# Weight loads two chunks ahead of the modulation blocks, and blocks moved behind LayerNorm, in a two-layer trunk

## The chip, the cores and the metric

The kernel runs on one core of a Trainium2 chip. The metric is the time of one execution on the device in microseconds, as the median of several runs. The profile is of one such execution; its times are counted from the first instruction.

The engines have these short names: PE is TensorE (PEld its weight loads), DVE is VectorE, ACT is ScalarE, POOL is GpSimd, SP is SyncE, which here issues all DMAs, in its program's order. Each engine runs its own list of instructions in order and waits at semaphores for the others.

## What is computed

Two layers of a trunk over 512 tokens of width 2048, in float32. Each layer:

```
mod = silu(c) @ ada_w[l] + ada_b[l]; shift, scale, gate = split(mod, 3)
h = rms_norm(x, norm_g[l]) * (1 + scale) + shift
z = h @ w_in[l]          # q-latent | kv-latent | rope key | MLA gate | conv input (2x) | conv gate
mla_out  = attention(q, k, v) * silu(mla_gate)        # 8 heads, low rank q and kv, causal
u = val * sigmoid(u_gate); u = depthwise_conv31(u)
u = silu(layer_norm(u)) @ w_pw[l] + b_pw[l]
conv_out = u * silu(conv_gate)
x = x + gate * (concat(mla_out, conv_out) @ w_out[l])
```

What matters here: `mod` is a product of a vector of 2048 with a matrix of 2048 x 6144 per layer. It needs 48 MB of weights in each layer and is done on VectorE. Of its 48 blocks of 128 values, blocks 0 to 15 are the shift, 16 to 31 the scale and 32 to 47 the gate, each for one chunk of 128 features.

## The kernel before

Features lie on the partitions in 16 chunks of 128, and tokens along the free axis, 512 of them. Products keep float32's precision: weights and activations are split into a high half (rounded to the matmul's format) and a low half (the rest), and each product takes three matmuls, high by high (L249), high by low (L250) and low by high (L251). Weights come as raw tiles of 512 KB (`load_w`, L228, four buffers). `split_w` (L235) makes the high half with a cast on ScalarE (L242, five buffers `hi`) and the low half with a subtraction (L243, five buffers `lo`), on GpSimd in most places; in the second layer's pointwise and output products (`PENG`, L94) on VectorE.

**A modulation block** (`Gemv.block`, L332) loads one block of 128 x 2048 weights (1 MB, tensor `ada`) and multiplies and sums it on VectorE in one instruction (L336), whose result is one column of `mod`. There are three buffers for these in the first layer's input product and two (`GB`) in the later stages. `make_h` (L352) makes a chunk of `h`: VectorE scales x (L356), ScalarE adds the shift and rounds (L357), VectorE makes the low half (L358).

**The input product of the first layer** (L442 to L459) goes over chunks of `h`: three for the first eight output tiles, then eight for the gate tiles `mg`, then the other thirteen for the first eight. `modulate_to` (L434) makes the chunks of `h` that the next step needs, with two blocks each, and `chunk` (L397) then loads 512 KB of weights, splits them and does 24 matmuls. **In the second layer** (L485 to L494) a chunk of `h` needs no block of its own at first; 14 blocks that the first layer left over (`LATE`) are done between the chunks, from the list `todo`.

**Behind attention** (L870 on), with the convolution's results ready, come the conv gate's product `cg` (8 tiles), the pointwise product `pw` (8 tiles) and the output product `wo` (16 tiles). LayerNorm's steps over the convolution are spread between the steps of `cg`: `ln_mean` (L876), `ln_center` (L881: subtract the mean, square on ScalarE, add into `vacc`), the token sums of `vacc` by matmuls (`st`, L194), the reciprocal root, `crs`, and `ln_silu` (L889), LayerNorm's last stage. `more(n)` (L910) puts blocks of `todo` between these: one per tile of `cg` once any instruction of LayerNorm is noted in `ln_ins`, one in each of the first six steps of `pw` behind the split of `cat`, and the rest at an even `rate` in the first 15 steps of `wo`. 34 blocks are done in this part in the first layer, 16 in the second.

The order in which instructions stand is set by a scheduler that takes the program's order and the dependences; `tc.issue_after(x)` holds an instruction behind x.

```
raw = load_w(src, 8, P)
for q in (0, 4):
    hi, lo = split_w(raw[:, q:q + 4], SENG)
    for n in range(4):
        mm3(tiles[q + n], hi[:, n], lo[:, n], hj[:, 0], hj[:, 1], start, stop)
```

Of the kernel before, what the change touches and what calls it, by code (L numbers as in the profile page):

```python
# [16 lines left out]
P = 128  # L17
S = 512
D = 2048
KC = D // P  # L20
NT = S // P
DEPTH = 2
H = 8
# [27 lines left out]
def hybrid_trunk(ctx, tc, xT, c, pos, invf, vec, adaT, w_s, w_t, w_kr, w_q, w_kv, w_pw, w_o, outT):  # L51
    nc = tc.nc
    V, A, T = nc.vector, nc.scalar, nc.tensor
# [16 lines left out]
    def nm(s):  # L70
        uid[0] += 1
        return f"{s}_{uid[0]}"
# [17 lines left out]
    AHEAD, NRAW, NHI, NLO = 2, 4, 5, 5  # L90
# [8 lines left out]
    K1, KH = 3, 8  # L99
# [6 lines left out]
    def psum(tag, n):  # L106
        return pp.tile([P, S], F32, tag=tag, bufs=NB[tag], name=nm(n))
# [11 lines left out]
    def ms(n):  # L119
        return f2(n, "m", NM)  # L120
# [107 lines left out]
    def load_w(src, a, b):  # L228

        raw = wp.tile([P, 1024], F32, tag="raw", bufs=NRAW, name=nm("raw"))  # L230
        rawv = raw[:, :a * b].rearrange("p (a b) -> p a b", a=a)
        nc.sync.dma_start(out=rawv, in_=src)
        return rawv
# [154 lines left out]
    def layer(l, xs, rstd, rpsum):  # L388
        last = l == DEPTH - 1
# [4 lines left out]

        tags = [t for t in ("mm", "up", "s", "cv", "pz") for _ in range(NB[t])]

        def chunk(tiles, src, hj, start, stop):  # L397
            raw = load_w(src, 8, P)
            for q in (0, 4):
                hi, lo = split_w(raw[:, q:q + 4], SENG)  # L400
                for n in range(4):
                    mm3(tiles[q + n], hi[:, n], lo[:, n], hj[:, 0], hj[:, 1], start, stop)
# [14 lines left out]
        def w_first(j):  # L417
            return w_s[l, j].rearrange("p (a b) -> p a b", a=8)

        h, part = [], [None] * H  # L420
        if l == 0:
            def modulated(j):
                if j >= EARLY:
                    scale0(j)
                g.block(0, j)
                h.append(make_h(0, j, xs[j], rstd if j else rpsum[0]))

            def park(tiles, where):
                for n in range(8):
                    p = where(n)  # L430
                    (A.copy if n % 2 else V.tensor_copy)(out=p, in_=tiles[n])
                    yield p

            def modulate_to(m):  # L434
                while len(h) < min(int(m), KC):
                    if len(h) < NI:
                        with tc.issue_after(rstd_ins.ins):
                            modulated(len(h))
                    else:
                        modulated(len(h))  # L440

            first = [psum(t, "z") for t in tags]  # L442
            for j in range(K1):
                modulate_to(j + 1)
                chunk(first, w_first(j), h[j], j == 0, j == K1 - 1)
            held = list(park(first, lambda n: ms("held") if n < 2 else f2("held", "held", 6, sp)))
            mg = [psum(t, "z") for t in tags]
            for j in range(KH):
                modulate_to(max(j + 1, K1 + MR0 * (j + 1)))
                chunk(mg, w_t[l, 0:H, :, j, :].rearrange("a p b -> p a b"), h[j], j == 0, j == KH - 1)  # L450
            part = list(park(mg, lambda n: ms("part")))
            first = [psum(t, "z") for t in tags]
            for j in range(K1, KC):
                modulate_to(max(j + 1, K1 + MR0 * KH + MR * (j + 1 - K1)))
                chunk(first, w_first(j), h[j], j == K1, j == KC - 1)
            krw = kr_weights()
            for n in range(8):
                V.tensor_add(out=held[n], in0=first[n], in1=held[n])
                first[n] = held[n]  # L459
        else:  # L460


            ws = []
            for j in range(2):
                raw = load_w(w_first(j), 8, P)
                ws.append([split_w(raw[:, q:q + 4], SENG, extra[0] if j and q else None) for q in (0, 4)])
                h.append(r4("h"))
            first = [psum(t, "z") for t in tags[:7]]

            def early(n, tk):  # L470
                for j in range(2):
                    hi, lo = ws[j][n // 4]
                    mm3(first[n][:, tk], hi[:, n % 4], lo[:, n % 4], h[j][:, 0, tk], h[j][:, 1, tk], j == 0, False)

            for i, (tk, rs) in enumerate(zip(HALF, rpsum)):
                for j in range(2):
                    make_h(l, j, xs[j], rs if j == 0 else rstd[:, tk], h[j], tk)
                for j in range(2):
                    for n in range(7):
                        hi, lo = ws[j][n // 4]  # L480
                        mm3(first[n][:, tk], hi[:, n % 4], lo[:, n % 4], h[j][:, 0, tk], h[j][:, 1, tk], i == 0 and j == 0, False)
            first.append(psum(tags[7], "z"))
            early(7, slice(0, S))
            h_ins = bc_ins[1]
            for j in range(2, KC):  # L485

                while len(todo) > max(KC, KC + 2 * (KC - LATE) - (j - 1) - max(0, min(2, j - 3))):
                    with tc.issue_after(h_ins.ins):
                        _, b = todo[0]
                        gemv[0].block(*todo.pop(0))  # L490
                        if b < KC:
                            make_gs(l, b)
                h.append(make_h(l, j, xs[j], rstd))
                chunk(first, w_first(j), h[j], False, j == KC - 1)  # L494
            krw = kr_weights()


# [375 lines left out]
        mean, vacc, crs = ms("mean"), ms("vacc"), ms("crs")  # L873
        ctile, ln_ins = [], [None]
# [6 lines left out]
        def ln_center(j):  # L881
            if j % 2 == 0:
                t = bp.tile([P, 2, S], F32, tag="c", bufs=4, name=nm("c"))
                nc.sync.dma_start(out=t, in_=cd[j // 2])
                ctile.extend((t[:, 0], t[:, 1]))
            ln_ins[0] = V.tensor_sub(out=ctile[j], in0=ctile[j], in1=mean)
            square_sum(vacc, ctile[j], j)

        def ln_silu(j):  # L889
# [35 lines left out]
        for j in range(NCC):  # L925
            for _ in range(4):
                ws.step()
                bg(VBUD)
            if ln_ins[0] is not None:
                with tc.issue_after(ln_ins[0].ins):  # L930
                    more(1)
        bg(1e9)
# [9 lines left out]
        def cat_split(src, t=None):  # L942
            t = r4("cat") if t is None else t
            A.copy(out=t[:, 0], in_=src)  # L944
            cat_ins[0] = V.tensor_sub(out=t[:, 1], in0=src, in1=f(t[:, 0]))  # L945
            return t
# [11 lines left out]
        for j in range(NCC):  # L958
            ws.step()
            ws.step()  # L960
            if j < 6:

                t = bp.tile([P, 2, S], F32R, tag="c", bufs=4, name=nm("cat")) if j < 4 else None
                cat[j] = cat_split(mout[j], t)
                with tc.issue_after(cat_ins[0].ins):
                    more(1)
        for j in (6, 7):
# [139 lines left out]
```

## Time and profile before

| | |
|---|---|
| median of 3 runs | 1667.66 us (1665.26 to 1672.59) |
| the profiled execution | 1668.02 us |
| its span, first to last instruction | 1666.2 us |
| TensorE busy | 1581.1 us (95%) |
| VectorE busy | 1226.2 us (74%) |
| ScalarE busy | 687.4 us (41%) |
| GpSimd busy | 659.7 us (40%) |
| granted clock of TensorE, mean | 0.987 |
| moved by DMA | 271.53 MB, mean 163 GB/s |

A matmul's shown duration overlaps the next one's, so TensorE counts as busy also where it is slow; how fast it goes is seen from the number of matmuls in a stretch, or from the distance of their starts. The chain of waits that ends last has 62% of its time on TensorE and 28% on VectorE, where the largest line is the block's, L336, with 7% of the span. The share of the granted clock is 1 at 2.4 GHz and 0.5 at 1.2 GHz.

### The profile page before, as it was taken

The page shows a single profiled execution, that of the slowest core. Times are in us where ns is not written, and L with a number is a line of the kernel's source. Part 1 is how long each engine was busy: PE and PEld are TensorE (multiplying, and loading weights), DVE is VectorE, ACT ScalarE, POOL GpSimd, SP SyncE. Part 2 cuts the span into 40 slices and gives each one's busy share as a digit, 9 for nine tenths or more (in the row PEclk, how much of TensorE's full clock was granted, in tenths as well). Part 3 has the DMA queues.
Part 4 walks back from the last instruction along what each step waited for, and adds up shares of the span by engine and source line. Part 5 has one row for each costly group of instructions (what it writes and reads, how often), then busy time and mean ns, then how long its engine had stood idle before and what let it go on. Part 6 is the DMA issues. An engine that isn't in the chain of part 4 may idle for free.

```text
span 1666.2 us, 20654 instructions
## 1 busy us (share of the span) xinstructions
PE 1581.1 (95%) x7350; PEld 1300.9 (78%) x7350; DVE 1226.2 (74%) x2008; ACT 687.4 (41%) x1284; POOL 659.7 (40%) x440
## 2 busy tenths in 40 slices
PE   4988999999999989999999899999999998999999
PEld 2766778877888878788887678888787887888888
DVE  8898897889999558766549675777788787784332
ACT  4222455554654335322223264545445443532221
POOL 2565633425233455666625554331434335100000
PEclk9999999999999999999999999999999999999999
DMA  8877323223233644898936613322332355565441
GB/s 304 287 278 286 135 90 100 70 83 86 76 114 98 231 152 167 287 335 296 322 98 228 246 64 108 92 92 80 99 93 70 104 170 211 177 236 198 151 142 62
DMA packets 82890, 271.53 MB, mean 163 GB/s; under 512 B 10721, under 2 KB 21729, under 8 KB 70241
## 3 DMA queue, kind: packets, MB, share of 16 engines
q1 hardware_dynamic: 82786, 270.20, 48.1%
q8 instruction: 58, 0.95, 0.2%
q14 instruction: 46, 0.38, 0.1%
HBM read 257.55 MB, written 12.62 MB: 162 GB/s over the span
## 4 chain that ended last, share of the span: by engine, by line
PE 62%; DVE 28%; ACT 6%; issue 3%; DMA 1%; POOL 1%; SPq 0%; POOLq 0%; ACTq 0%; DVEq 0%
DVE ada L336 7%; PE wo L250 7%; PE wo L251 7%; PE wo L249 7%; DVE cv L547 5%; PE z L249 4%; PE z L251 4%; PE z L250 4%; PE cg L249 3%; PE cg L251 3%; PE cg L250 3%; PE mg L251 2%; PE mg L249 2%; PE mg L250 2%; DVE x L356 2%
## 5 line engine op out<-in xcount | busy, mean ns | idle before, releaser
L243 POOL TENSOR_TENSOR lo<-raw,hi 128x512 fp32r<-128x512 f32 x380 | 595.2, 1581 | 657.5 <-ACT hi L242 647.3
L242 ACT CAST hi<-raw 128x512 fp32r<-128x512 f32 (+1 forms) x512 | 307.1, 611 | 518.0 <-PE wo L250 209.6
L547 DVE SCALAR_TENSOR_TENSOR cv<-u,lvec,cv 128x512 f32<-128x512 f32 x464 | 348.6, 751 | 7.4
L249 PE MATMUL z<-h,hi 128*128 128x512 f32 (+1 forms) x782 | 305.8, 396 | 17.2 <-ACT h L357 11.0
L251 PE MATMUL z<-h,lo 128*128 128x512 f32 (+1 forms) x782 | 305.8, 391 | 8.3 <-POOL lo L243 8.3
L250 PE MATMUL z<-h,hi 128*128 128x512 f32 (+1 forms) x782 | 304.6, 390 | 0.8 <-DVE h L358 0.7
L336 DVE CUSTOM_DVE_ANT_0 ada<-ada,cb,avec 128x2048 f32<-128x2048 f32 x96 | 257.4, 2682 | 40.5 <-DMA ada<-in_adaT_dram 40.4
L249 PE MATMUL wo<-cat,hi 128*128 128x512 f32 (+1 forms) x544 | 205.8, 378 | 2.0 <-ACT cat L944 2.0
L250 PE MATMUL wo<-cat,hi 128*128 128x512 f32 (+1 forms) x544 | 206.3, 379 | 1.1 <-DVE cat L945 1.0
L251 PE MATMUL wo<-cat,lo 128*128 128x512 f32 (+1 forms) x544 | 205.8, 378 | 0.0
L249 PEld LDWEIGHTS z<-h,hi 128*128 128x128 f32 x782 | 148.5, 191 | 49.2 <-ACT h L357 13.4
L251 PEld LDWEIGHTS z<-h,lo 128*128 128x128 f32 x782 | 148.4, 190 | 42.9 <-POOL lo L243 13.3
L250 PEld LDWEIGHTS z<-h,hi 128*128 128x128 f32 x782 | 148.6, 190 | 29.3 <-DVE h L358 1.8
L243 DVE TENSOR_TENSOR lo<-raw,hi 128x512 fp32r<-128x512 f32 (+1 forms) x132 | 86.3, 655 | 95.0 <-ACT hi L242 94.7
L249 PEld LDWEIGHTS wo<-cat,hi 128*128 128x128 f32 x544 | 102.9, 189 | 21.2 <-ACT cat L944 2.4
L250 PEld LDWEIGHTS wo<-cat,hi 128*128 128x128 f32 x544 | 102.9, 189 | 21.2 <-DVE cat L945 2.3
L251 PEld LDWEIGHTS wo<-cat,lo 128*128 128x128 f32 x544 | 103.0, 189 | 18.8
L249 PE MATMUL cg<-h,hi 128*128 128x512 f32 x256 | 103.0, 402 | 0.0
L250 PE MATMUL cg<-h,hi 128*128 128x512 f32 x256 | 101.5, 397 | 0.0
L251 PE MATMUL cg<-h,lo 128*128 128x512 f32 x256 | 101.5, 396 | 0.0
L780 ACT ACTIVATE pr<-pr,smx,sc 128x128 f32<-128x128 f32 (+1 forms) x64 | 41.9, 654 | 122.8 <-DVE smx L779 122.7
L357 ACT ACTIVATE h<-x,mod 128x512 fp32r<-128x512 f32 (+1 forms) x34 | 23.3, 697 | 136.8 <-DVE mod L336 100.5
(265 smaller groups left out, 2543.4 us busy)
## 6 DMA issues: line engine op xcount, KB each, us to landing
ada<-in_adaT_dram SPq DMA_DIRECT2D x96, 1024.0 KB, 5.7
raw<-in_w_t_dram SPq DMA_DIRECT2D x120, 512.0 KB, 3.8
raw<-in_w_o_dram SPq DMA_DIRECT2D x64, 512.0 KB, 4.6
raw<-in_w_s_dram SPq DMA_DIRECT2D x32, 512.0 KB, 5.9
raw<-in_w_pw_dram SPq DMA_DIRECT2D x16, 512.0 KB, 3.6
raw<-in_w_q_dram SPq DMA_DIRECT2D x24, 256.0 KB, 2.7
x<-in_xT_dram SPq DMA_DIRECT2D x8, 512.0 KB, 6.8
kf<-kfd SPq DMA_DIRECT2D x16, 256.0 KB, 3.7
```

The source lines that it names most:

```text
L242: A.copy(out=hiv, in_=rawv)
L243: i = eng.tensor_tensor(out=lov, in0=rawv, in1=f(hiv), op=ALU.subtract)
L249: T.matmul(out=ps, lhsT=whi, rhs=mhi, start=start, stop=False)
L250: T.matmul(out=ps, lhsT=whi, rhs=mlo, start=False, stop=False)
L251: T.matmul(out=ps, lhsT=wlo, rhs=mhi, start=False, stop=stop)
L336: V.tensor_tensor_reduce(out=t, in0=t, in1=self.cb, scale=1.0, scalar=vv(l, "ada_b", b), op0=ALU.mult, op1=ALU.add, accum_out=mods[l][:, b ...
L356: V.scalar_tensor_tensor(out=x, in0=x, scalar=gs(l, j), in1=rstd, op0=ALU.mult, op1=ALU.mult)
L357: A.activation(out=hi, in_=x, func=AF.Identity, bias=shift(l, j))
L547: V.scalar_tensor_tensor(out=box[-1], in0=u[:, k:k + S], scalar=w, in1=box[0], op0=ALU.mult, op1=ALU.add)
L780: A.activation(out=pr[:, :n], in_=pr[:, :n], func=AF.Exp, scale=scl, bias=nb, accum_out=sums)
```

## The change

Three things change.

1. Weights of the input products are loaded ahead. A list `to_come` holds the loads still to be issued, in order, and `come(n)` issues them until `n` loaded tiles stand ready. In the first layer `come(AHEAD)`, with `AHEAD` = 2, is called ahead of the blocks of each new chunk of `h` (but the first), in the second ahead of the blocks of each chunk from the third on. `chunk` takes the oldest loaded tile.
2. `ln_center` no longer notes its instruction in `ln_ins`, so the blocks in `cg` begin behind the first `ln_silu`. In the second layer there are none in `cg`.
3. In the pointwise product the first layer's blocks stand in steps 1 to 5 instead of 0 to 5, and the second layer has none. As `rate` shares out what is left, the first layer's output product gets 28 blocks instead of 24, and the second's 16, all that there are.

```diff
-        def chunk(tiles, src, hj, start, stop):
-            raw = load_w(src, 8, P)
+        raws, to_come = [], []
+
+        def come(n):
+
+            while to_come and len(raws) < n:
+                raws.append(load_w(to_come.pop(0), 8, P))
+
+        def chunk(tiles, hj, start, stop):
+            come(1)
+            raw = raws.pop(0)
...
                     else:
+                        come(AHEAD)
                         modulated(len(h))
 
+            to_come += [w_first(j) for j in range(K1)]
+            to_come += [w_t[l, 0:H, :, j, :].rearrange("a p b -> p a b") for j in range(KH)]
+            to_come += [w_first(j) for j in range(K1, KC)]
...
-                chunk(first, w_first(j), h[j], j == 0, j == K1 - 1)
+                chunk(first, h[j], j == 0, j == K1 - 1)
...
             h_ins = bc_ins[1]
+            to_come += [w_first(j) for j in range(2, KC)]
             for j in range(2, KC):
+                come(AHEAD)
...
-            ln_ins[0] = V.tensor_sub(out=ctile[j], in0=ctile[j], in1=mean)
+            V.tensor_sub(out=ctile[j], in0=ctile[j], in1=mean)
...
-            if ln_ins[0] is not None:
+            if ln_ins[0] is not None and not last:
                 with tc.issue_after(ln_ins[0].ins):
                     more(1)
...
                 cat[j] = cat_split(mout[j], t)
+            if 0 < j < 6 and not last:
                 with tc.issue_after(cat_ins[0].ins):
                     more(1)
```

Where the instructions now stand, at three places.

VectorE, first layer, the end of the sum over LayerNorm's squares (`vacc`), up to the first use of its token sums (`st`); before, with two of the blocks (`ada`):

```order
L370 TENSOR_TENSOR vacc_4650<-vacc_4650,sq_5138 128x512
L336 ISA ada_5186,mod_122<-ada_5186,cb_4652,avec_120 128x2048
L336 ISA mod_122 128x1
L370 TENSOR_TENSOR vacc_4650<-vacc_4650,sq_5162 128x512
L336 ISA ada_5275,mod_122<-ada_5275,cb_4652,avec_120 128x2048
L336 ISA mod_122 128x1
L370 TENSOR_TENSOR vacc_4650<-vacc_4650,sq_5166 128x512
L215 TENSOR_SCALAR sm_5224<-st_5225 128x4
```

and now:

```order
L900 TENSOR_TENSOR c_5156<-c_5156,mean_4649 128x512
L370 TENSOR_TENSOR vacc_4650<-vacc_4650,sq_5135 128x512
L370 TENSOR_TENSOR vacc_4650<-vacc_4650,sq_5159 128x512
L370 TENSOR_TENSOR vacc_4650<-vacc_4650,sq_5163 128x512
L215 TENSOR_SCALAR sm_5218<-st_5219 128x4
```

The additions follow each other, and no block stands between the mean and the token sums.

ScalarE, first layer, the first chunks of the input product: casts of weights (`hi`, from `raw`) and the chunks of `h`; before:

```order
L222 COPY rstd_37_208<-stb_41_226 128x512
L357 ACTIVATE h_52_247<-x_15_144,mod_3_122 128x512
L242 CAST hi_62_298<-raw_61_296 128x512
L242 CAST hi_64_314<-raw_61_296 128x512
L357 ACTIVATE h_60_292<-x_15_144,mod_3_122 128x512
L242 CAST hi_70_343<-raw_69_341 128x512
L242 CAST hi_72_359<-raw_69_341 128x512
L357 ACTIVATE h_68_337<-x_17_150,mod_3_122 128x512
```

and now:

```order
L222 COPY rstd_37_208<-stb_41_226 128x512
L242 CAST hi_63_300<-raw_58_285 128x512
L242 CAST hi_65_316<-raw_58_285 128x512
L357 ACTIVATE h_52_247<-x_15_144,mod_3_122 128x512
L242 CAST hi_71_345<-raw_59_287 128x512
L242 CAST hi_73_361<-raw_59_287 128x512
L242 CAST hi_91_401<-raw_67_332 128x512
L357 ACTIVATE h_62_296<-x_15_144,mod_3_122 128x512
```

The casts of one or two chunks now stand ahead of the `h` that they stood behind.

SyncE, second layer, loads of weight tiles (`raw`) and blocks (`ada`) in the input product; the weights of chunk 11 are `raw_1400` before:

```order
L335 DMA ada_1384_7573<-in_adaT_dram 128x2048
L232 DMA raw_1393_7622<-in_w_s_dram 128x1024
L335 DMA ada_1391_7615<-in_adaT_dram 128x2048
L335 DMA ada_1398_7656<-in_adaT_dram 128x2048
L232 DMA raw_1400_7664<-in_w_s_dram 128x1024
```

and `raw_1392` now:

```order
L335 DMA ada_1379_7536<-in_adaT_dram 128x2048
L232 DMA raw_1385_7575<-in_w_s_dram 128x1024
L335 DMA ada_1386_7577<-in_adaT_dram 128x2048
L232 DMA raw_1392_7617<-in_w_s_dram 128x1024
L335 DMA ada_1393_7619<-in_adaT_dram 128x2048
```

Ahead of the load for chunk 11 stand eight loads of blocks of this stage instead of ten.

## Rows read from the trace of the kernel before

**Rows 1.** Windows: busy us (instructions) of PE, PEld, DVE, ACT, POOL; PEclk, DMA share, GB/s

```profile
34.00:187.00 153.00, 136.30 (x555) 107.21 (x556) 136.26 (x114) 41.51 (x73) 90.44 (x46) 0.98 0.77 274
...
608.00:620.00 12.00, 7.75 (x25) 6.13 (x24) 7.16 (x14) 0.90 (x2) 6.12 (x3) 0.72 0.71 263
...
690.00:740.00 50.00, 50.00 (x218) 41.28 (x217) 32.97 (x31) 13.58 (x22) 35.39 (x18) 0.98 0.93 329
...
1420.00:1488.00 68.00, 68.00 (x306) 56.45 (x304) 55.63 (x72) 33.54 (x57) 7.03 (x5) 1.00 0.62 216
```

**Rows 2.** Waits of PE, whole run: waited for, us in total, times, longest

```profile
PE st L194 <- DVE vacc L370: 8.5, 2, 4.2
...
PE wo L249 <- ACT cat L944: 2.0, 1, 2.0
PE wo L250 <- DVE cat L945: 1.0, 1, 1.0
```

**Rows 3.** Timeline of DVE, first layer's LayerNorm: start us, us, instruction [idle before]

```profile
591.82 2.34 DVE L336 CUSTOM_DVE_ANT_0 ada<-ada,cb,avec 128x2048 f32<-128x2048 f32 x1
...
603.99 2.34 DVE L336 CUSTOM_DVE_ANT_0 ada<-ada,cb,avec 128x2048 f32<-128x2048 f32 x1
...
607.96 3.37 DVE L336 CUSTOM_DVE_ANT_0 ada<-ada,cb,avec 128x2048 f32<-128x2048 f32 x1
...
611.26 1.74 DVE L370 TENSOR_TENSOR vacc<-vacc,sq 128x512 f32<-128x512 f32 x1
```

**Rows 4.** Timeline of PE at the same place

```profile
613.05 1.68 PE L194 MATMUL st<-ones,vacc 128*128 128x1 f32 x8 [4.25 <-DVE vacc L370]
614.59 0.77 PE L249 MATMUL cg<-h,hi 128*128 128x512 f32 x1
...
620.21 0.40 PE L250 MATMUL cg<-h,hi 128*128 128x512 f32 x1
```

**Rows 5.** Timeline of PE, second layer's LayerNorm

```profile
1414.39 0.77 PE L249 MATMUL cg<-h,hi 128*128 128x512 f32 x1
...
1418.80 0.41 PE L250 MATMUL cg<-h,hi 128*128 128x512 f32 x1
```

**Rows 6.** Timeline of PE, first tile of the first layer's output product

```profile
682.41 0.39 PE L251 MATMUL wo<-cat,lo 128*128 128x512 f32 x1
...
691.99 0.40 PE L250 MATMUL wo<-cat,hi 128*128 128x512 f32 x1
```

**Rows 7.** Timeline of DVE, the end of the first layer's pointwise product

```profile
677.46 3.38 DVE L336 CUSTOM_DVE_ANT_0 ada<-ada,cb,avec 128x2048 f32<-128x2048 f32 x1
...
682.80 0.74 DVE L953 SCALAR_TENSOR_TENSOR y<-pw,lvec,cg 128x512 f32<-128x512 f32 x1
```

**Rows 8.** Timelines of ACT and PE, second layer's input product

```profile
932.86 0.62 ACT L242 CAST hi<-raw 128x512 fp32r<-128x512 f32 x1 [5.09 <-DMA raw<-in_w_s_dram]
...
933.53 0.50 PE L249 MATMUL z<-h,hi 128*128 128x512 f32 x1 [1.69 <-ACT hi L242]
...
935.77 0.50 PE L251 MATMUL z<-h,lo 128*128 128x512 f32 x1 [1.51 <-POOL lo L243]
```

**Rows 9.** First layer's input product: PE's waits (34 to 187 us), timelines of ACT and PE

```profile
PE z L249 <- ACT h L357: 10.4, 4, 3.3
...
41.66 0.73 ACT L357 ACTIVATE h<-x,mod 128x512 fp32r<-128x512 f32 x1 [6.41 <-DVE mod L336]
...
42.21 0.39 PE L251 MATMUL z<-h,lo 128*128 128x512 f32 x1
```

**Rows 10.** Timeline of DVE, late tiles of the first layer's output product

```profile
808.77 0.74 DVE L1018 SCALAR_TENSOR_TENSOR x<-wo,mod,xr 128x512 f32<-128x512 f32 x1
...
821.26 0.74 DVE L1018 SCALAR_TENSOR_TENSOR x<-wo,mod,xr 128x512 f32<-128x512 f32 x1
...
826.65 0.75 DVE L1018 SCALAR_TENSOR_TENSOR x<-wo,mod,xr 128x512 f32<-128x512 f32 x1 [3.25 <-PE wo L251]
```

**Rows 11.** POOL's subtractions by line: count, ns min/median/max, first and last start

```profile
L243 POOL TENSOR_TENSOR lo<-raw,hi x380: 1256/1295/3450, 24.1 to 1433.7; 128x512 fp32r<-128x512 f32 x190
```

More of the change, by code (lines that the diff above doesn't have):

```diff
@@ L449, in layer @@
                 modulate_to(max(j + 1, K1 + MR0 * (j + 1)))
-                chunk(mg, w_t[l, 0:H, :, j, :].rearrange("a p b -> p a b"), h[j], j == 0, j == KH - 1)
+                chunk(mg, h[j], j == 0, j == KH - 1)
             part = list(park(mg, lambda n: ms("part")))
@@ L454, in layer @@
                 modulate_to(max(j + 1, K1 + MR0 * KH + MR * (j + 1 - K1)))
-                chunk(first, w_first(j), h[j], j == K1, j == KC - 1)
+                chunk(first, h[j], j == K1, j == KC - 1)
             krw = kr_weights()
@@ L493, in layer @@
                 h.append(make_h(l, j, xs[j], rstd))
-                chunk(first, w_first(j), h[j], False, j == KC - 1)
+                chunk(first, h[j], False, j == KC - 1)
             krw = kr_weights()
```

## The prediction

> **What bounds the kernel now.** I read the busy times by stage first, then who waited for whom, then the timelines of the places that the change touches. TensorE is at its full rate almost everywhere: between 1420 and 1488 us it starts 306 matmuls in 68 us, 0.222 us each, and that is the floor of every stage built of 512-column matmuls [rows 1]. The change can only give back stretches in which TensorE falls short of that. Four of them lie where instructions move.
>
> The first two are alike, one in each layer. In the product for the convolution gate, TensorE comes to the sum over LayerNorm's squares (`st`) and finds `vacc` unfinished: 8.5 us in two waits [rows 2]. In the first layer VectorE had run three modulation blocks between the LayerNorm steps, and finished `vacc` behind the last of them [rows 3]. The wait is 4.25 us, and after it the clock is at the lower of its two levels, 1.2 GHz, for some microseconds (0.72 granted on average from 608 to 620 us [rows 1]): the 13 matmuls from 614.59 to 620.21 us take 5.62 us instead of 13 x 0.222 = 2.89 [rows 4]. The second layer repeats it: ten matmuls take 4.41 us instead of 2.22 [rows 5].
>
> Third, the first tile of the first layer's output product: TensorE waits 2.0 and 1.0 us for `cat` [rows 2], the clock falls again, and 14 matmuls take 9.58 us instead of 3.11 [rows 6]. ACT writes the awaited `cat` behind the last `y`, and VectorE makes that at 682.80, one of six blocks in its pointwise product just ahead of it [rows 7].
>
> Fourth, the second layer's input product: at 932.86 ScalarE starts a cast for which it waited 5.09 us on a weight load, and TensorE stands 1.69 us for that and 1.51 us for its low half [rows 8].
>
> The first layer's input product is another case. TensorE starts 555 matmuls in 153 us there, 123 us of work at 0.222, so it is 30 us short [rows 1]; but VectorE is busy 136 of these 153 us, TensorE's largest wait is for `h`, 10.4 us [rows 9], and VectorE's own work does not shrink. This stage is VectorE's.
>
> **The change part by part.**
>
> *LayerNorm.* Blocks leave the centring steps in both layers. On VectorE's path to `vacc` the first layer loses three blocks of 2.34, 2.34 and 3.37 us, 8.05 us together [rows 3]; TensorE waits 4.25 [rows 4]. So `vacc` is ready before TensorE asks, and the lower clock goes with the idle time. That gives 4.25 + 5.62 - 2.89 = 7.0 us in the first layer, and 4.25 + 4.41 - 2.22 = 6.4 in the second, whose wait is the other half of the 8.5 [rows 2, 4, 5]. Late next would be the squares from ScalarE, which stands in order behind casts that wait for TensorE; the lowest value is nothing, if these hold `vacc` as long as the blocks did. I take the full value, since 8.05 us of work leave and only 4.25 are needed.
>
> *Pointwise product, first layer.* One of its six blocks goes (five are left ahead of the last `y`), 3.38 us by the row of its last one [rows 7]. TensorE's two waits are 3.0 us [rows 2], so they nearly vanish. Of the 9.58 - 3.11 = 6.5 us lost around them [rows 6] I count 5.5, because the last two low halves of `cat` still follow each other closely. The bounds are 2.5 (waits shorter, clock still low) and 6.5.
>
> *Output product, first layer.* Four blocks come to it: 28 instead of 24, so two per tile in nearly all of the first 14 tiles, where before some had one and the last three none. TensorE lost nothing between 690 and 740 us, where tiles already have two blocks, with VectorE busy 33 and GpSimd 35 of 50 us [rows 1]. This cover is the reason for pricing it at nothing. It isn't wide: DMA moves 329 GB/s at a share of 0.93 [rows 1], and VectorE runs late when such tiles follow each other, as the rivals show. Bounds: 0 and 10 us lost.
>
> *Output product, second layer.* All 16 gate blocks stand here, about one per tile. VectorE splits the weights in it, so a block that waits for its load holds splits back; but one block of 2.34 us [rows 3] per tile of 48 x 0.222 = 10.7 us has its two buffers filled a tile ahead. Nothing, bounds 0 and 2 lost.
>
> *Weights ahead, second layer.* SyncE issues loads in order, and a block's load waits until VectorE frees its buffer. The load for chunk 11 stood behind ten blocks of this stage and now stands behind eight. That takes away the two waits behind it, 1.69 + 1.51 = 3.2 us [rows 8]. The stage is TensorE's at its end, so they count in full. Other waits here are of casts behind an `h` that is late itself, and their order stays. Bounds: 0 and 6.
>
> *Weights ahead, first layer.* Casts move in front of the `h` they stood behind; VectorE's order is the same but for the first `h`. Gains are possible only behind the last `h`, about 1 us. There is a loss at the start: the cast now ahead of the second `h` needs a buffer that TensorE frees with the first chunk, whose last matmul starts at 42.21 us, while that `h` ran at 41.66 [rows 9]. The difference of 0.55 and the matmul's own 0.39 us put it 0.9 us later, with the cast on top, less what the first chunk gains because its low half of `h` now comes before a block. I take 1 us lost. And TensorE, with its casts done, idles in one piece before each late `h`; two falls of the clock at the price of [rows 4], 2 x 2.7 us, would make it 5.4 lost. Bounds: 2 gained and 5.4 lost. The Trainium skill (TensorE: Matmul & The Clock Gate, HAM oscillation — how this bites in real kernels) warns against just such bunched idle gaps, a rule against casting ahead; by it the sum would be 4.4 us higher. By that rule the trace agrees behind the `vacc` waits; the clock of this whole stage is 0.98 [rows 1], so I keep the smaller price.
>
> The sum: the profiled execution took 1668.0 us (span 1666.2), 0.4 above the median. 1668.0 - 7.0 - 6.4 - 5.5 - 3.2 + 1.0 = 1646.9 us, given as **1647 us**, 1.2% faster.
>
> **The rivals.**
>
> *ScalarE holds the statistic.* Without the blocks, `vacc` waits for squares behind casts. For it: ScalarE is in order and waits on TensorE in this stage. Against: the price of the missing blocks is twice the wait. Half of the two LayerNorm gains would stay out: 1647 + 6.7 = 1654 us.
>
> *VectorE falls behind in the first layer's output product.* With two blocks per tile, its tile outputs at 808.77 and 821.26 us are 12.49 us apart, while the product makes one in 10.7, so 1.8 us are lost per tile [rows 10]. Over 13 tiles that is 23 us. It decides once the lag exceeds the lead of the weight loads, which now queue behind the store of an output; a tile is about 10.7 us, so some 10 to 12 us reach TensorE: 1658 us. Against: at 826.65 VectorE waited for TensorE again, one tile without blocks later [rows 10], and with two per tile around 690 to 740 nothing was late.
>
> *Casts hold `h` in the whole first stage.* If every `h` of the 15 behind the first came 1 us late, and VectorE with it: 1647 + 14 = 1661 us. Against: later casts ask for buffers that TensorE freed long before.
>
> *Splits become the bound (slower than before).* GpSimd subtracts four times per tile in the first layer's output product, at 1.295 us the median and 3.45 the longest [rows 11]. If all four took 3.45 us, a tile would take 13.8 instead of 10.7, and 13 tiles 40 us more: 1687 us. It decides when three of four are held up: 3 x 3.45 + 1.3 = 11.6 is over 10.7, while two make 9.5. For it: blocks and subtractions do lengthen each other. Against: two blocks per tile can hold up two subtractions, and GpSimd was busy 35 of 50 us with as many [rows 1]. The Trainium skill (SBUF — State Buffer, Who interferes with whom) has a rule for it: VectorE with two SBUF inputs and GpSimd exclude each other for a whole instruction; the longest subtraction, 3.45, is close to 1.3 plus a block's 2.34, as that rule has it.
>
> *The loads don't run ahead*, as blocks still stand between them in the queue: 1650 us, inside the range.
>
> **How the numbers follow.** The forecast with its small terms (1641 to 1652) gets 0.66; ScalarE 0.11; VectorE behind 0.12; casts 0.05; splits 0.06. The range goes from 1640, where the pointwise and weight terms reach their upper bounds, to 1660, which takes in the first two rivals and leaves out the last two: 0.11, and a few hundredths at the lower end. A change under 0.5%, 8.3 us, can't be told from none. Faster by that means under 1659.3: 0.66 + 0.11 + most of 0.12 = 0.86. Within: 0.07, for the casts and the rest of the lag. Slower: 0.07, the splits and what I overlooked.
>
> **What would show it.** Right: no wait for `vacc` in either layer and a full clock behind; `cat` waits under 1 us at the first output tile; no 5 us wait of a cast for a weight load in the second input product; 28 and 16 blocks in the output products with TensorE still at 0.222 us. Wrong: `st` waiting for squares, matmuls of either output product waiting for a low half or a cast, a first input product that takes longer than now, or clock falls in it that cost more than the casts bring.

## The result, and the profile after

The changed kernel takes **1645.46 us** (median, 1644.57 to 1646.07). The kernel before took 1668.65 us beside it. The ratio is 0.986, with a 95% interval of 0.9837 to 0.9883. The forecast was 1647 us, between 1640 and 1660. The profiled execution has a span of 1643.7 us instead of 1666.2, so 22.5 us went. Ratios here compare fast executions; one of the ten of the kernel with 34 blocks took 8905.54 us and is left out of its ratio.

Where they went is read from the starts of the same matmuls in both traces: the first one of each stage. The middle columns are what each stage adds to or takes from the time between the two.

| stage, by TensorE's first matmuls | predicted | this pair of traces | other traces with the same order there |
|---|---|---|---|
| start of the first product | – | +0.3 | -1.2 to +1.2 |
| first input product | +1.0 | +3.6 | +0.3 to +4.5 (six) |
| first layer's LayerNorm, in `cg` | -7.0 | -7.7 | -7.7 |
| `pw` and first tile of `wo` | -5.5 | -5.9 | -5.9 to -6.5 |
| first layer's `wo`, second tile to last | 0 | 0.0 | 0.0 |
| second input product | -3.2 | -1.7 | -1.7 or -1.8 |
| second layer's attention | – | -3.8 | -3.1 to -3.8, or 0.0 in two |
| second layer's LayerNorm, in `cg` | -6.4 | -7.4 | -7.4 |
| second layer's `wo` | 0 | 0.0 | 0.0 |

The windows of the changed kernel, with the columns of [rows 1]; the one at 1390 us is at the second layer's LayerNorm:

```profile
34.00:187.00 153.00, 137.77 (x552) 108.93 (x552) 136.66 (x112) 40.07 (x69) 92.83 (x48) 0.96 0.77 271
608.00:620.00 12.00, 12.00 (x59) 10.03 (x58) 3.10 (x11) 3.15 (x6) 5.58 (x5) 1.00 0.33 100
690.00:740.00 50.00, 50.00 (x223) 41.38 (x222) 36.71 (x30) 12.60 (x21) 32.25 (x17) 1.00 0.93 333
1390.00:1402.00 12.00, 12.00 (x59) 10.03 (x58) 2.83 (x10) 2.98 (x5) 5.16 (x4) 1.00 0.34 114
```

From 608 to 620 us TensorE starts 59 matmuls instead of 25, at the full clock instead of 0.72. In the first input product it starts three fewer than before in the same 153 us, at 0.96 instead of 0.98. Where the output product now has two blocks per tile, it still starts 223 in 50 us.

TensorE's waits in the whole run; those for `vacc` [rows 2] are gone from the list, and `cat` is down from 3.0 us to 0.2, while the wait for `h` has grown (10.4 us in the first input product before [rows 9]):

```profile
PE z L249 <- ACT h L357: 18.6, 10, 4.8
PE wo L250 <- DVE cat L959: 0.2, 1, 0.2
```

The timeline of VectorE and then of TensorE at the first layer's token sums, where [rows 3] and [rows 4] were:

```profile
604.00 4.27 DVE L370 TENSOR_TENSOR vacc<-vacc,sq 128x512 f32<-128x512 f32 x3
613.59 0.16 DVE L215 TENSOR_SCALAR sm<-st 128x4 f32<-128x4 f32 x1 [5.32 <-PE st L194]
```

```profile
612.60 0.94 PE L194 MATMUL st<-ones,vacc 128*128 128x1 f32 x8
613.41 0.49 PE L249 MATMUL cg<-h,hi 128*128 128x512 f32 x1
```

`vacc` is ready at 608.27 us, 4.3 us before TensorE asks for it. Now VectorE is the one that waits. `st` itself takes 0.94 us instead of 1.68.

The second layer's input product: TensorE's last wait in it, then ScalarE's last chunk of `h` with the casts behind it, in the changed kernel and in the kernel before.

```profile
940.73 0.50 PE L251 MATMUL z<-h,lo 128*128 128x512 f32 x1 [0.69 <-POOL lo L243]
```

```profile
938.02 0.72 ACT L357 ACTIVATE h<-x,mod 128x512 fp32r<-128x512 f32 x1 [7.78 <-DVE mod L336]
938.65 2.16 ACT L242 CAST hi<-raw 128x512 fp32r<-128x512 f32 x4
```

```profile
944.83 0.72 ACT L357 ACTIVATE h<-x,mod 128x512 fp32r<-128x512 f32 x1 [1.76 <-DVE mod L336]
945.46 2.17 ACT L242 CAST hi<-raw 128x512 fp32r<-128x512 f32 x4
```

The 5.09 us wait of a cast for its weights [rows 8] is gone, and with it 3.2 us of TensorE's. But TensorE loses 1.5 us around 940 us that it did not lose before. Four casts follow the last `h` in both kernels; now that `h` stands 84.6 us behind the stage's first matmul instead of 81.8, and TensorE, which is early, has to wait for the casts and low halves behind it. VectorE, which makes the values for the last two chunks of `h`, has two longer blocks there, in the changed kernel (first fence) than in the kernel before (second fence):

```profile
924.55 3.37 DVE L336 CUSTOM_DVE_ANT_0 ada<-ada,cb,avec 128x2048 f32<-128x2048 f32 x1
...
929.39 3.38 DVE L336 CUSTOM_DVE_ANT_0 ada<-ada,cb,avec 128x2048 f32<-128x2048 f32 x1
```

```profile
932.25 2.35 DVE L336 CUSTOM_DVE_ANT_0 ada<-ada,cb,avec 128x2048 f32<-128x2048 f32 x1
...
937.16 2.42 DVE L336 CUSTOM_DVE_ANT_0 ada<-ada,cb,avec 128x2048 f32<-128x2048 f32 x1 [0.89 <-DMA ada<-in_adaT_dram]
```

Beside the two longer ones GpSimd runs subtractions, which now come in pieces of three and four. (Where a subtraction starts behind the block, as the one at 933.56 us in the kernel before, it is the subtraction that is longer, 2.16 us.)

```profile
918.18 7.59 POOL L243 TENSOR_TENSOR lo<-raw,hi 128x512 fp32r<-128x512 f32 x4 [4.17 <-ACT hi L242]
929.27 5.89 POOL L243 TENSOR_TENSOR lo<-raw,hi 128x512 fp32r<-128x512 f32 x3 [3.50 <-ACT hi L242]
```

### The profile page after: what moved, and what is told of

Its sections match the earlier page's. It is cut to its first block, busy times and chain, and to the rows that moved or that the text cites. A ratio compares the mean times of both kernels' runs of the same rounds, so it can differ in the third digit from the quotient of the medians.

```text
span 1643.7 us, 20668 instructions
## 1 busy us (share of the span) xinstructions
PE 1571.4 (96%) x7350; PEld 1294.4 (79%) x7350; DVE 1232.7 (75%) x2008; ACT 686.7 (42%) x1284; POOL 653.3 (40%) x440
## 4 chain that ended last, share of the span: by engine, by line
PE 64%; DVE 23%; ACT 6%; issue 4%; POOL 2%; DMA 0%; SPq 0%; POOLq 0%; ACTq 0%; DVEq 0%
PE wo L250 7%; PE wo L251 7%; PE wo L249 7%; DVE cv L561 6%; DVE ada L336 5%; PE z L250 4%; PE z L251 4%; PE z L249 4%; PE cg L251 3%; PE cg L249 3%; PE cg L250 3%; POOL lo L243 2%; PE pw L250 2%; PE pw L251 2%; PE pw L249 2%
## 5 line engine op out<-in xcount | busy, mean ns | idle before, releaser
L243 POOL TENSOR_TENSOR lo<-raw,hi 128x512 fp32r<-128x512 f32 x380 | 586.2, 1558 | 637.3 <-ACT hi L242 616.8
L249 PEld LDWEIGHTS z<-h,hi 128*128 128x128 f32 x782 | 148.5, 191 | 51.2 <-ACT h L357 22.5
L249 PE MATMUL cg<-h,hi 128*128 128x512 f32 x256 | 101.0, 394 | 0.0
L250 PE MATMUL cg<-h,hi 128*128 128x512 f32 x256 | 99.8, 390 | 0.0
L251 PE MATMUL mg<-h,lo 128*128 128x512 f32 x192 | 76.2, 397 | 2.3 <-POOL lo L243 2.3
```

The lines of the kernel that those rows point to most:

```text
L243: i = eng.tensor_tensor(out=lov, in0=rawv, in1=f(hiv), op=ALU.subtract)
L249: T.matmul(out=ps, lhsT=whi, rhs=mhi, start=start, stop=False)
L250: T.matmul(out=ps, lhsT=whi, rhs=mlo, start=False, stop=False)
L251: T.matmul(out=ps, lhsT=wlo, rhs=mhi, start=False, stop=stop)
```

## The experiments

All are edits of the changed kernel, but for the one that is the kernel before. The first four take the change apart.

**Loading ahead in the second layer only.**

```diff
                     else:
-                        come(AHEAD)
                         modulated(len(h))
```

> The first layer's input product loads each chunk's weights at the chunk again; everything else as in the changed kernel. Theory (casts ahead of h, and what they bring, cost the stage 3.6 us; the rest of the gain does not depend on it): the product ends at 193.4 us instead of 197.2, TensorE's waits for h in the stage fall from 18.6 to 10.4 us, and the time is 1645.5 - 3.6 = 1641.9 us. Rival (clock falls are drawn anew in every kernel, and the stage was only unlucky): the product ends anywhere from 193 to 198 us, or the 3.6 us come back as a clock fall later on, and the time is 1645 us.

Measured: 1645.46 us, ratio 0.9862 [0.9846, 0.9878]. The first stage was short again, 158.7 us from its first matmul to its last (159.0 before, 162.6 in the changed kernel). But the first layer's attention became 1.8 us longer with a fall of the clock at 394 us. The stage came out as the theory has it, the time as the rival has it.

**Loading ahead alone**, in both layers, with the blocks where they stood before.

```diff
-            V.tensor_sub(out=ctile[j], in0=ctile[j], in1=mean)
+            ln_ins[0] = V.tensor_sub(out=ctile[j], in0=ctile[j], in1=mean)
...
-            if ln_ins[0] is not None and not last:
+            if ln_ins[0] is not None:
...
-            if 0 < j < 6 and not last:
+            if j < 6:
```

> The kernel before, with only the weights loaded ahead, in both layers; LayerNorm and the pointwise product have their blocks as before. Theory (the parts add up; the second layer's input product gains 1.7, the first layer's loses 3.6, and the 2.7 us clock fall at 996 us in the second layer's attention is tied to when that stage begins, not to this change): 1668.6 + 3.6 - 1.7 = 1670.5 us, waits for vacc still about 8 us. Rival (loading ahead also brings the second attention's 3.8 us): 1666.7 us.

Measured: 1665.19 us, ratio 0.9983 [0.9969, 0.9996]. The number is nearer the rival's. The second input product gave 1.7 us as expected, the first lost only 0.4, and the second attention was 3.1 us shorter. TensorE's waits for `vacc` are all there:

```profile
PE st L194 <- DVE vacc L370: 8.5, 2, 4.3
```

**The blocks alone**, with no loading ahead.

```diff
                     else:
-                        come(AHEAD)
                         modulated(len(h))
...
             for j in range(2, KC):
-                come(AHEAD)
```

> The changed kernel without any loading ahead, in either layer; only the blocks are moved. Theory (parts add up: 7.7 us in the first LayerNorm, 5.9 in the pointwise product and its first output tile, 7.4 in the second LayerNorm): 1668.6 - 21.0 = 1647.6 us, and the second layer's input product is back at its old length of 99.8 us; less by 2.7 if the clock does not fall in the second attention. Rival (loading ahead is what makes the second layer's gain): 1651 us, with 3.8 us more in the second attention.

Measured: 1646.48 us, ratio 0.9871 [0.9854, 0.9888]. That is the theory's 1647.6 with some of the 2.7. The second input product is as long as before, to 0.01 us, and the second attention is 3.2 us shorter here too, without any loading ahead. So nearly the whole gain comes with the moved blocks. The 3.2 us of the attention are in it; as the kernel with loading ahead alone has 3.1 us of the same, they belong to neither part by itself.

**Six blocks in the pointwise product.**

```diff
-            if 0 < j < 6 and not last:
+            if j < 6 and not last:
```

> The changed kernel with six blocks again in the first layer's pointwise product, in its steps 0 to 5, and so 27 in the output product. Theory (the block just ahead of the last y makes the last cat late, and the idle time lowers the clock): the first output tile takes 5.9 us longer, TensorE waits 2 to 3 us for cat there, 1651.4 us. Rival (the first tile is late because the last two low halves of cat follow each other, whatever the blocks): unchanged, 1645.5 us.

Measured: 1651.20 us, ratio 0.9897 [0.9883, 0.9912], against 1651.4 expected. One block, and both waits at the first output tile are back, with the low clock behind them:

```profile
679.08 0.50 PE L249 MATMUL wo<-cat,hi 128*128 128x512 f32 x1 [1.99 <-ACT cat L958]
680.77 0.79 PE L250 MATMUL wo<-cat,hi 128*128 128x512 f32 x1 [1.19 <-DVE cat L959]
...
686.46 0.63 PE L250 MATMUL wo<-cat,hi 128*128 128x512 f32 x1
```

**Two blocks back into LayerNorm's centring**, first layer.

```diff
-            V.tensor_sub(out=ctile[j], in0=ctile[j], in1=mean)
+            ctr = V.tensor_sub(out=ctile[j], in0=ctile[j], in1=mean)
+            if j >= 6:
+                ln_ins[0] = ctr
```

> The changed kernel with two blocks back ahead of the last two additions into vacc in the first layer (of the three that the change took out). Theory (vacc is ready 4.3 us before TensorE asks for it in the changed kernel; two blocks of 2.3 to 3.4 us take 4.7 to 6.8): TensorE waits 0.4 to 2.5 us for vacc, and if that idle time lowers the clock 2.7 us come on top; 1646 to 1650.5 us. Rival (squares or something else held vacc, and the blocks run in their shadow): no wait, 1645.5 us.

Measured: 1648.92 us, ratio 0.9882 [0.9866, 0.9897]. VectorE has the two blocks between its last additions, and TensorE, in the second fence, waits 0.92 us:

```profile
602.62 2.34 DVE L336 CUSTOM_DVE_ANT_0 ada<-ada,cb,avec 128x2048 f32<-128x2048 f32 x1
...
606.59 3.37 DVE L336 CUSTOM_DVE_ANT_0 ada<-ada,cb,avec 128x2048 f32<-128x2048 f32 x1
...
609.89 1.76 DVE L370 TENSOR_TENSOR vacc<-vacc,sq 128x512 f32<-128x512 f32 x1
```

```profile
611.71 1.05 PE L194 MATMUL st<-ones,vacc 128*128 128x1 f32 x8 [0.92 <-DVE vacc L370]
```

The clock did not fall here, and the LayerNorm stage lost 1.1 us of its 7.7. So 5.7 us of blocks against a slack of 4.3 cost about their difference, and the price of the three blocks was a step beyond it: an idle time of 4.25 us, and the clock [rows 4]. Most of the rest of its longer time is, in its trace, a clock fall in the second attention (3.1 us), of which more below.

**All 34 blocks in the first layer's output product.**

```diff
-            if ln_ins[0] is not None and not last:
-                with tc.issue_after(ln_ins[0].ins):
-                    more(1)
...
-            if 0 < j < 6 and not last:
-                with tc.issue_after(cat_ins[0].ins):
-                    more(1)
```

> The changed kernel with no block between the conv gate's or the pointwise product's steps in the first layer: all 34 in its output product, 2.3 per tile, six more than now. Theory (the output product is near DMA's limit: it moves 53.7 MB in 163.7 us at a share of 0.92; six blocks bring 6.3 MB, and at the highest rate seen in a slice of it, 338 GB/s, 60.0 MB take 177 us): 14 us longer less the 1 us by which the pointwise product may shrink, 1658 us, with waits for the weights of the output product. Rival (VectorE and GpSimd have room and DMA goes up to the 363 GB/s seen elsewhere): 1.6 us longer, 1647 us. A third (VectorE falls behind and the tiles' outputs hold the weights): tile outputs over 11.5 us apart, 1655 us or more.

Measured: 1667.69 us, ratio 1.000 [0.9986, 1.0014]. Six blocks take the whole gain of the change away. The trace is of an execution of 1672.85 us. In it the product takes 177.5 us from the start of its second tile to that of its last, instead of 152.3, and TensorE waits 12.5 us for casts there and 2.4 us for low halves. The windows, with the columns of [rows 1], and what SyncE waited for between 670 and 870 us:

```profile
720.00:770.00 50.00, 44.56 (x181) 35.24 (x180) 28.24 (x26) 11.35 (x20) 27.63 (x16) 0.93 0.87 326
770.00:820.00 50.00, 44.53 (x186) 35.35 (x185) 34.63 (x27) 11.55 (x20) 26.66 (x18) 0.97 0.90 325
```

```profile
SPq L335 <- DVE mod L336: 66.0, 22, 6.7
SPq L1028 <- DVE x L1027: 61.7, 15, 8.1
```

The first theory had the size wrong and the limit too: at 326 GB/s DMA moves less than the changed kernel's 333. VectorE has work for 28 to 35 of 50 us. In the changed kernel SyncE's two waits of the same kinds are 66.5 and 43.6 us, so it is the one for the tile's output that grew. The rows read as a ring. On VectorE (first fence) a block that waits for its load stands in front of the tile's output at 713.50. SyncE (second fence) holds its queue at that output's store (L1028), then at the second of two block loads until VectorE has done the block at 715.73; behind both stand the next weights, at 719.01. ScalarE (third fence) waits 8.55 us for these, and TensorE 2.74 us, up to 727.31, for the cast:

```profile
710.91 2.67 DVE L336 CUSTOM_DVE_ANT_0 ada<-ada,cb,avec 128x2048 f32<-128x2048 f32 x1 [0.62 <-DMA ada<-in_adaT_dram]
...
713.50 0.74 DVE L1027 SCALAR_TENSOR_TENSOR x<-wo,mod,xr 128x512 f32<-128x512 f32 x1
...
715.73 2.35 DVE L336 CUSTOM_DVE_ANT_0 ada<-ada,cb,avec 128x2048 f32<-128x2048 f32 x1
```

```profile
714.27 0.33 SPq L1028 DMA_DIRECT2D x1d<-x  x1
714.65 3.80 SPq L335 DMA_DIRECT2D ada<-in_adaT_dram  x2
...
719.01 1.29 SPq L232 DMA_DIRECT2D raw<-in_w_o_dram  x2
```

```profile
726.63 1.14 ACT L242 CAST hi<-raw 128x512 fp32r<-128x512 f32 x2 [8.55 <-DMA raw<-in_w_o_dram]
```

**The same with three buffers for the blocks' weights**, to break that ring.

```diff
-    GB, GC = 2, 15
+    GB, GC = 3, 15
```

> The kernel with all 34 blocks in the first layer's output product, with three buffers for block weights instead of two. Theory (a ring: a block waits for its load, the tile's output stands behind the block, the store of that output holds SyncE's queue, and behind the store stand the next weights; one more buffer lets a block's load start a block earlier): waits of TensorE for casts there fall from 12.5 us to under 4, the product takes 163 to 172 us up to its last tile instead of 188, and 1648 to 1655 us. Rival (the transfers themselves are the limit, 60 MB at 300 to 338 GB/s): 177 us or more, and 1658 us or more.

Measured: 1665.17 us, ratio 0.9974 [0.9963, 0.9986]. The theory missed: TensorE's waits for casts fell from 12.5 to 7.6 us, not under 4. The product's time up to its last tile fell from 188.4 to 178.4 us, so in these traces the third buffer takes 10 of 25 us back. The median fell by 2.5 us only; in this trace, against that of the run before, the first input product is 4.2 us longer, the second 1.6 (its stage has the third buffer too), and the second attention, with a fall of the clock, 3.0. SyncE's waits for a free buffer nearly went; those for the tile's output grew:

```profile
SPq L1028 <- DVE x L1027: 105.1, 15, 10.3
...
SPq L335 <- DVE mod L336: 12.8, 8, 3.0
```

178.4 us is the rival's number (177 or more). But from 690 to 740 us, where TensorE loses nothing, DMA moves 334 GB/s here, and in the windows with the losses 327 or less. Whether the rest is the transfers or the store's place in the queue stays open; a store on another queue wasn't tried. So the ring is shown in part, by the buffer's 10 us, and otherwise argued from the rows.

**Casts behind `h`.** Loads ahead as in the change, but the first layer's casts held behind the newest chunk of `h`.

```diff
-        A.activation(out=hi, in_=x, func=AF.Identity, bias=shift(l, j))
+        h_act[0] = A.activation(out=hi, in_=x, func=AF.Identity, bias=shift(l, j))
...
-                hi, lo = split_w(raw[:, q:q + 4], SENG)
+                with tc.issue_after(h_act[0].ins) if l == 0 else ExitStack():
+                    hi, lo = split_w(raw[:, q:q + 4], SENG)
```

> The changed kernel, in which the first layer's weights are loaded ahead as now, but their casts on ScalarE are held behind the newest chunk of h, as they nearly all stood before. Theory (the casts' place ahead of h is what costs the first stage): the stage ends at 193 to 194 us as without loading ahead, TensorE's waits for h there near 10 us instead of 18, and 1643 us. Rival (the place of the casts costs under 1 us, the rest is clock falls that come with any order): the stage ends between 193 and 198 us, with falls at other places, and the time stays 1645.5 within 1.5 us.

Measured: 1648.66 us, ratio 0.9886 [0.987, 0.9902]; the stage took 165.0 us, longer than in any other kernel. Both expectations missed. The waits for `h` are gone, and TensorE waits for the casts and low halves instead (34 to 198 us):

```profile
PEld z L251 <- POOL lo L243: 16.0, 20, 1.1
...
PE z L249 <- ACT hi L242: 11.5, 8, 1.8
```

So holding every cast behind `h` is worse than either order. This edit holds back more casts than the old order did, so it does not isolate the change's.

**Loading ahead from the fourth chunk on.**

```diff
                     else:
-                        come(AHEAD)
+                        if len(h) >= K1:
+                            come(AHEAD)
                         modulated(len(h))
```

> The changed kernel, in which the first layer loads ahead only from the fourth chunk of h on; the first three chunks' weights come at their chunk, as before. Theory (in the seven traces with this stage's two orders, loading ahead makes the second h 1.9 us and the fourth 1.7 to 2.9 us later, from the casts ahead of them and the second chunk's products, and gives 1.4 to 2.5 us back behind the last h): the fourth h stands 28 to 29.5 us behind the first matmul, the last 150 to 151, and the stage takes 157 to 158 us instead of 159.3 to 162.6; 1643 us. Rival (the later h are late by their own casts, wherever the start is): the last h at 152 to 154 us all the same, 1645.5 us.

Measured: 1647.43 us, ratio 0.9873 [0.9857, 0.9889]. The theory missed: the second and third `h` are on time, but the fourth stands 32.1 us behind the first matmul and the stage takes 163.9 us. The scheduler moved something else. VectorE copies four of the first tiles (`held`) here ahead of the next block, not two, and each copy waits for TensorE, 0.46 to 2.23 us:

```profile
58.10 0.69 DVE L439 COPY held<-z 128x512 f32<-128x512 f32 x1 [0.67 <-PE z L251]
58.71 2.34 DVE L336 CUSTOM_DVE_ANT_0 ada<-ada,cb,avec 128x2048 f32<-128x2048 f32 x1
```

In the kernel before, that block ran at 54.73 us. The question of the start is not decided by this run; what it shows is how much a block behind a TensorE wait costs in this stage.

**The two kernels once more**, for second traces.

> The kernel before once more, for a second trace of the same program. Theory (some clock falls are not set by the program's order but drawn anew in each execution; the one at 996 us is such a one): this trace lacks it or has others, and its stages otherwise agree within 0.5 us; 1665 to 1668 us. Rival (the fall at 996 us belongs to the kernel before, as four changed kernels lack it): it is there again.

> The changed kernel once more, for a second trace and more times. Theory (the 3.6 us that its first stage lost hold about 1 us of order and the rest clock falls drawn anew): the stage ends at 194 to 196 us here, as in the two other kernels with the same order there (194.1 and 195.2). Rival (the loss belongs to the order): it ends at 197 us again. Either way the median stays at 1645.5 within 1 us.

The kernel before: 1668.0 us, all stages within 0.75 us of the first trace, and the fall at 996 us is there again, as the rival had it. The changed kernel: 1645.96 us, ratio 0.9871 [0.9855, 0.9888]; its first stage took 161.2 us (162.6 in the first trace) and ended at 195.7, as the theory has it, and its second attention has no fall again.

**Loading ahead in the second layer only, once more**, as a candidate.

> The kernel that loads ahead in the second layer only, once more, as the candidate for the best version. Theory (its first input product takes 158.3 to 159.0 us as in the four traces with that order, 1 to 3 us less than the changed kernel's; the 1.8 us fall of the clock at 394 us in its first trace comes and goes): 1643 us in the median, and the stage at 159 us. Rival (what the stage gains is lost again elsewhere, as in its first runs): 1645.5 us.

Measured: 1643.96 us, ratio 0.9848 [0.9834, 0.9862]. The interval overlaps that of the changed kernel, and its first runs gave 1645.46. It may be about 1 us faster; these runs can't tell it apart. The 394 us fall is in its second trace too.

## Why the prediction was right

The sum of 21.1 us was right because its large terms were. That it came within 1.5 us of the 22.6 between the spans is in part luck: in this pair of traces the first stage, the second input product and the start miss by 4.4 us to the slow side, and the two LayerNorms, the pointwise product and an attention that the prediction does not have by 5.9 to the fast side. The floor of 0.222 us per matmul counts short matmuls too (the pointwise product's 192 take 43.5 us, 0.227 each); this moves no term by more than 0.1 us.

- **LayerNorm, -7.0 and -6.4: right, a little small.** Measured -7.7 and -7.4. The mechanism is as written: the blocks were on the path, `vacc` is early now, and the clock stays. The rival in which ScalarE's squares hold `vacc` did not come. What the term left out is `st`, which also ran at the lower clock: 1.68 us then, 0.94 now in the first layer, and 1.87 and 0.95 in the second. With two of the three blocks back the wait was 0.92, which bears out "8.05 leave and only 4.25 are needed".
- **Pointwise product, -5.5: right.** Measured -5.9, and putting the block back cost 5.7 (1651.20 - 1645.46).
- **First layer's output product, 0: right, but on a narrow cover.** In all traces with 28 blocks it lost 0.0. VectorE did fall behind, by up to 4.9 us, as in [rows 10], and recovered. Six more blocks cost 25 us. The rival "VectorE falls behind" was therefore a real cliff; its place was beyond two blocks per tile, not at it. GpSimd's subtractions, the rival with 1687 us, took little part even there: POOL was busy 27 to 28 of 50 us, and TensorE waited 2.4 us for low halves.
- **Second layer's output product, 0: right.**
- **Second input product, -3.2: mis-sized.** Measured -1.7. The two waits went in full, and behind them TensorE was 3.3 us ahead of the kernel before, counted from the stage's first matmul. But the step "the stage is TensorE's at its end, so they count in full" failed: TensorE, early now, meets the last `h`, which VectorE makes 2.8 us later in the stage than before, and 1.5 us come back there.
- **First input product, +1.0: mis-sized, and its mechanism was wrong.** Seven traces with the changed order took 159.3 to 163.5 us, mean 161.0; five with the old order 158.3 to 159.6, mean 158.9. So it costs 2.1 us, within the bounds. The term had the second `h` wait for a cast that waits for TensorE. That cast does wait (2.50 us), but `h` then still waits for VectorE:

```profile
42.87 0.62 ACT L242 CAST hi<-raw 128x512 fp32r<-128x512 f32 x1 [2.50 <-PE z L250]
43.93 0.72 ACT L357 ACTIVATE h<-x,mod 128x512 fp32r<-128x512 f32 x1 [0.44 <-DVE mod L336]
```

VectorE, in the same stretch, waits for the first `h` ahead of its low half, where it ran a block before, and its next two blocks are 1 us longer each (2.34 and 2.35 in the kernel before). The low half itself is 1.0 us shorter (0.75 instead of 1.76), so about 1.9 us are left:

```profile
34.58 0.75 DVE L358 SCALAR_TENSOR_TENSOR h<-x,mod,h 128x512 fp32r<-128x512 f32 x1 [0.91 <-ACT h L357]
35.25 3.36 DVE L336 CUSTOM_DVE_ANT_0 ada<-ada,cb,avec 128x2048 f32<-128x2048 f32 x1
...
40.48 3.41 DVE L336 CUSTOM_DVE_ANT_0 ada<-ada,cb,avec 128x2048 f32<-128x2048 f32 x1
```

GpSimd's earlier subtractions run beside both, three from 33.49 us on and one at 40.45. The Trainium skill (SBUF — State Buffer, Who interferes with whom) has VectorE with two SBUF inputs and a GpSimd instruction that reads SBUF exclude each other; these rows agree, a block being longer by 1.02 to 1.06 us where a subtraction of some 1.3 us [rows 11] runs beside it. In all seven traces the second `h` stands 9.3 us behind the first matmul instead of 7.4, and the last one 152.4 to 154.9 instead of 149.6 to 151.7, while the stretch behind the last `h` takes 6.9 to 8.5 us instead of 7.8 to 9.4. The gain that the term expected there is real: 6.9 us instead of 7.8 in traces without a fall of the clock in that stretch, 8.5 instead of 9.4 with one. "VectorE's order is the same but for the first `h`" was true, and was not enough: what runs beside it changed. How the last `h` comes some 3 us later, when the second is 1.9 late, is not shown for the rest. The granted clock from 34 to 187 us is 0.93 to 0.96 in the seven traces and 0.96 to 0.98 in the five, but within the seven the stage's length does not follow it (159.3 us at 0.93, 162.6 at 0.96). The Trainium skill (TensorE: Matmul & The Clock Gate, HAM oscillation — how this bites in real kernels) warns against bunched idle gaps; the sum by it was 4.4 us higher, and the measured 1.1 us above the term lies between it and mine.

- **Not in the prediction: the second attention, -3.8.** No instruction of it moves. It is a clock fall that the kernel before has and the changed one hasn't, for 3.1 us, and a wait for `pt` at 1287 us that is 0.39 us in this trace instead of 1.08. The fall is shown below. Without it the forecast would have been some 2 us too low, still within the range.

## What to carry to other kernels

Movable work on an engine that TensorE waits for belongs behind the statistic or the last input that TensorE needs, and its price ahead of it is a step: nothing up to the slack (4.3 us here), the excess beyond it (1.1 us for 5.7 us of blocks), and with three blocks, at a wait of 4.25 us, the low clock too. Where it is moved to, ask not only for the busy shares but for the ring of queues: six blocks more made 25 us though DMA moved less than before (326 GB/s against 333) and VectorE was busy 28 to 35 of 50 us. And loads ahead of need pull casts and subtractions forward, which can lengthen the very engine that bounds the stage (here by 1.0 us for a block that starts beside a running subtraction).

## What was not expected of the hardware

After the same idle time of TensorE the clock is lower in one kernel and not in the next. In the second attention TensorE waits 1.00 us for `ksq`. The kernel before, then the changed one, then the kernel with two blocks in the centring:

```profile
994.30 1.05 PE L194 MATMUL st<-ones,ksq 64*128 64x1 f32 x8 [1.00 <-ACT ksq L834]
...
995.64 0.63 PE L250 MATMUL mg<-h,hi 128*128 128x512 f32 x1
996.07 0.63 PE L251 MATMUL mg<-h,lo 128*128 128x512 f32 x1
```

```profile
982.94 1.05 PE L194 MATMUL st<-ones,ksq 64*128 64x1 f32 x8 [1.00 <-ACT ksq L848]
...
984.26 0.40 PE L250 MATMUL mg<-h,hi 128*128 128x512 f32 x1
984.50 0.40 PE L251 MATMUL mg<-h,lo 128*128 128x512 f32 x1
```

```profile
982.59 1.05 PE L194 MATMUL st<-ones,ksq 64*128 64x1 f32 x8 [0.95 <-ACT ksq L848]
...
983.99 0.63 PE L250 MATMUL mg<-h,hi 128*128 128x512 f32 x1
984.41 0.63 PE L251 MATMUL mg<-h,lo 128*128 128x512 f32 x1
```

The matmuls ahead are the same, 0.227 us apart. Behind the wait they are 0.43 and 0.42 us apart in the first and third kernel, at the lower clock, and 0.24 in the second. Both traces of the kernel before and two of changed kernels have this fall, ten others lack it, and the third kernel's wait stands only 0.35 us from the second's. The wait at 394 us in the first layer is another such place: 2.07 us with a fall in the kernel that loads ahead in the second layer only, 2.08 without one in the changed kernel. Which it will be could not be read from any row, and no run here decides it. So of a difference of 2 to 4 us between two versions, one such fall may be all.
